# First feed-forward of a decoder block: modulation products, block sums of u and the depth of the weight split, moved in the order

## The chip, the cores and the metric

One core of a Trainium2 chip. The metric is device time in microseconds (us) of one execution of the program on that core. TensorE (PE, with its weight loads PEld) multiplies; VectorE (DVE), ScalarE (ACT) and GpSimd (POOL) compute beside it; SyncE (SP) issues nearly all loads, POOL the accumulating ones.

## The reference

One decoder block in float32, 512 tokens of width 1024. A vector c gives nine modulation vectors of 1024; three sublayers, each normed, shifted, scaled and gated by three of these, are added to the stream h, and a last norm ends it:

```python
cond = silu(c)
sh1, sc1, gt1, sh2, sc2, gt2, sh3, sc3, gt3 = split(cond @ w_ada + b_ada, 9)
u = rmsnorm(h, g1) * (1 + sc1) + sh1
h = h + 0.5 * gt1 * swiglu(u, w_ffn1_in, w_ffn1_out)     # (silu(a) * b) @ w_out, a, b = split(u @ w_in), D_FF = 2816
u = rmsnorm(h, g2) * (1 + sc2) + sh2
h = h + gt2 * token_mixing(u, ...)                       # pooling and dilated attention, gated
u = rmsnorm(h, g3) * (1 + sc3) + sh3
h = h + 0.5 * gt3 * swiglu(u, w_ffn2_in, w_ffn2_out)
return rmsnorm(h, g_final)
```

The change lies in the first swiglu.

## The kernel before, in words

**Layout.** Everything is transposed: features on the 128 partitions, the 512 tokens along the row. h lies in eight tiles H, u in eight pairs UH, UL. Each float32 operand is split into a high part, rounded to what a fast matmul takes (`hi`, on ACT), and the rest (`lo`, on DVE); a product is three matmuls: hi by hi, hi by lo, lo by hi.

**Weight chunks.** Weights come in chunks of 128 x 1024, loaded by SP (line 244) into a few buffers (raw0 to raw2, later also others that are idle: quarters of X, `kept1`, `G`) and split into a ring `whi`, `wlo` that holds seven chunks. `split_hi` makes, where a chunk is a difference of block weights, that difference on DVE (line 260), and the high part on ACT (line 321); `split_lo` the low part on DVE (line 335). For some chunks (`outer`) the low part is made otherwise: ACT writes the negative rounded copy into `wlo` (line 317), and POOL issues a load that adds the weights from memory to it (line 319). `look(n)` before each tile or product splits chunks until n stand ahead of the one in use; `take` hands the next one to TensorE. Chunks 0 to 7 are the startup's, 8 to 11 the plain pairs', 12 to 15 the first output part's, 16 to 22 the first block pair's seven products'.

**Stages of the first feed-forward.** The startup computes modulation rows 0 to 15 and norm, and the first eight tiles of u @ w_in (four pairs a, b, lines 1801 to 1805). Its end takes their results (`ffn_post`: the product silu(a) b into `kept` on DVE, line 671, the high part HI on ACT, line 680, the low part HK on DVE, line 681). Then two plain pairs, j = 4 and 5 (`ffn_pair`: two tiles each of 24 matmuls, lines 366 to 368). Then the first output part, eight tiles in four steps m = 0, 2, 4, 6, each tile added into H on DVE (line 1199). All further pairs go by a seven-product scheme on 2 x 2 blocks (Strassen's way; `duo`, two pairs at a time, from j = 6; `out_quad` for the output). It needs sums and differences of u's blocks (`u_steps`, lines 731 to 739: SH, SL from quarters of X; the last step overwrites parts of UH, UL) and of the weights' blocks (line 260). The sums of u wait in the list `todo` and are made one by one behind the H additions of the first output part; while `hold` is true, no weight difference is made ahead of time.

**Modulation rows.** Rows of w_ada (128 x 1024 each) are loaded by SP (line 381) and multiplied and summed on DVE (`ada_do`, line 389; `bg` does the next one and fetches more). Rows 16 to 23, the first feed-forward's gate, go beside the plain pairs from a pool of four buffers; `beside_out` closes that pool, opens the space of the u sums, and from then on rows go through the two buffers cs and AR, two per block pair, up to row 39.

**Order.** Each engine runs its instructions in the order in which this code issues them; nothing is reordered later. An instruction waits in its engine's queue until its inputs are there, and what is behind it waits too. Buffers are handed out in the order in which they come free, so a change in the order here exchanges raw buffers and quarters of X in the stages behind, too.

Of the kernel before, what the change touches and what calls it, by code (L numbers as in the profile page):

```python
# [125 lines left out]
PLAIN = {0: 6, 2: 2}  # L126
# [16 lines left out]
class Kernel:  # L143
# [279 lines left out]

    def beside(self, j, i):

        if self.nh == 4 and i in (2, 5):
            self.bg()

    def bg_fetch(self):
        while self.ada_ahead < min(self.ada_stop, self.ada_next + self.ada_depth) and self.ada_free != []:  # L430
# [342 lines left out]
    def duo(self, j, first):  # L773
# [32 lines left out]
        for i, (bank, u, start) in enumerate(((A, blk(lo4, T1), True), (B, S[0], True), (A, S[1], False),  # L806
                                              (C, blk(hi4, T1), False), (A, S[2], False), (B, S[3], False),
                                              (A, blk(hi4, T2), False))):
            if i == 6:
                v.tensor_tensor(c1, c1, u3, op=OP.add)  # L810
            self.look(3 + i // 3 if first else 5)
            self.product(bank, u, start)
            self.step()
            if i == 0:
                copy(C, A)
                if first:
                    first()
                    self.free.append(self.rawx[0])
            elif i == 1:
                copy(c1, r(B))  # L820
            elif i == 2:
                copy(c0, r(A))
            elif i == 3:
                silu(0, C)
            elif i == 4:
                copy(u3, r(A))
            elif i == 6:
                silu(1, A)
                v.tensor_tensor(c0, r(B), c0, op=OP.add)
            self.beside(j, i)  # L830
            if self.nh == 4 and j >= PARTS[-2][0] and self.todo:
                self.todo.pop(0)()
# [306 lines left out]
    def ffn(self, n, j, last=None):  # L1139
# [4 lines left out]
            self.banks, self.bi = list(self.B), 0  # L1144

        def beside():
            if n == 0:
                self.bg()
                if part == 0 or j == PLAIN[0] - 2:
                    self.bg()  # L1150

        for part, (k0, k1) in enumerate(PARTS[:-1]):
            while j < pairs_before(n, part):
# [3 lines left out]
                else:  # L1157
# [4 lines left out]
                    self.duo(j, last)  # L1162
                    last = None
                    j += 2
            if n == 0:
                last = self.beside_out(part) or last
            if part + 2 == len(PARTS):
                self.sums.close()
                if n:
# [13 lines left out]
            nk = k1 - k0  # L1183
            hk = [self.hh(k) for k in range(k0, k1)]
            for m in range(0, KT, 2):
                if m == 4:
                    self.bg_fetch()
                self.look(4 - m // 2)
                w = self.take()
                bs = [self.nb(), self.nb()]  # L1190

                for ka, kb in ((0, nk - 1), (nk - 1, nk)) if m == 0 else ():
                    for i in range(2):
                        for k in range(ka, kb):
                            self.mm3(bs[i], *w[nk * i + k], *hk[k], k == 0, k == nk - 1)
                for i, b in enumerate(bs):
                    for k in range(nk if m else 0):
                        self.mm3(b, *w[nk * i + k], *hk[k], k == 0, k == nk - 1)
                    v.scalar_tensor_tensor(self.H[m + i], b, gate[:, m + i:m + i + 1], self.H[m + i],
                                           op0=OP.mult, op1=OP.add)  # L1200
                    if self.todo:
                        self.todo.pop(0)()
                    if self.hold and not self.todo:
                        self.hold = False
                        self.look(2)
                self.step()
# [497 lines left out]
    def startup(self):  # L1704
# [99 lines left out]
            for (hi, lo), b in zip(w, banks):  # L1804
                M(b, lo, self.UH[k], start=False, stop=k == KT - 1)  # L1805
        self.ada_next = self.ada_ahead = 16
        self.ada_stop = 24
        self.bg_fetch()
        for j in range(FIRST):
            self.split(self.pos + j)  # L1810
            self.fetch()
            self.ffn_post(j, self.ffn_silu(j, banks[2 * j]), banks[2 * j + 1])


def constants():
# [55 lines left out]
```

## Time and profile before

| | us |
|---|---|
| median of three runs | 994.1 |
| lowest, highest | 989.12, 1396.78 |
| profiled execution | 993.37 |
| its span, first to last instruction | 991.6 |

| engine | busy us | share |
|---|---|---|
| PE | 977.8 | 99% |
| PEld | 921.3 | 93% |
| DVE | 830.4 | 84% |
| ACT | 591.5 | 60% |
| POOL | 95.6 | 10% |

The granted TensorE clock is 0.997 of full speed over the span. In lists in order of time the columns are the start in us from the span's beginning, the duration in us, the engine, the line, the operation and its tiles (written <- read); brackets give the idle time ahead and what ended it. Starts that lie closer than the durations mean pipelining. L770 is a block product, L366 to L368 a plain one.

### The profile page before, as it was taken

What the parts mean: (1) busy time and instruction counts of PE and PEld (TensorE: products, weight loads), DVE (VectorE), ACT (ScalarE), POOL (GpSimd) and SP (SyncE); (2) the same over time, 40 slices, a digit from 0 to 9 for tenths busy, and PEclk for the clock granted to TensorE, in tenths of its full rate; (3) what the DMA queues carried; (4) which work ended last, traced back from release to release, by engine and by line L of the source; (5) the groups of instructions that cost most, each with busy time, mean ns of one, the idle gap of its engine ahead of it and who ended that gap; (6) DMA issues with size and microseconds to landing.
All of it is one profiled execution on the core that took longest, in us unless ns stands there. A gap on an engine that the chain in (4) does not pass through costs nothing.

```text
span 991.6 us, 17667 instructions
## 1 busy us (share of the span) xinstructions
PE 977.8 (99%) x7106; PEld 921.3 (93%) x7106; DVE 830.4 (84%) x1246; ACT 591.5 (60%) x910; POOL 95.6 (10%) x107
## 2 busy tenths in 40 slices
PE   8999999999999999999999999999999999999997
PEld 7888999999999999889988888899999999999996
DVE  5979899999999877879666777479997988989876
ACT  5454687786868753333324333368876768577775
POOL 0000111111111100006200000000110010011001
PEclk9999999999999999999999999999999999999998
DMA  8959687877869822133265774346576566657622
GB/s 308 294 189 310 173 230 199 235 199 215 221 190 227 201 68 88 63 107 105 77 228 190 269 246 139 106 152 138 138 176 183 151 163 167 181 136 193 170 57 85
DMA packets 53636, 172.76 MB, mean 174 GB/s; under 512 B 6065, under 2 KB 11057, under 8 KB 53554
## 3 DMA queue, kind: packets, MB, share of 16 engines
q1 hardware_dynamic: 41778, 137.95, 40.6%
q0 software_dynamic: 11088, 33.04, 19.7%
q8 instruction: 55, 0.90, 0.4%
q10 hardware_dynamic: 688, 0.66, 0.2%
q14 instruction: 27, 0.22, 0.1%
HBM read 168.85 MB, written 2.77 MB: 173 GB/s over the span
## 4 chain that ended last, share of the span: by engine, by line
PE 94%; DVE 3%; ACT 1%; DMA 1%; issue 0%; DVEq 0%; ACTq 0%
PE bank L770 33%; PE bank L366 8%; PE bank L368 8%; PE bank L367 8%; PE bank L890 6%; PE bank L892 6%; PE bank L891 6%; PE bank L632 3%; PE bank L1801 1%; PE bank L1805 1%; PE bank L1803 1%; PE bank L1391 1%; PE bank L1572 1%; DMA wlo<-wf1i 1%; PE bank L1730 1%; PE bank L1573 1%
## 5 line engine op out<-in xcount | busy, mean ns | idle before, releaser
L335 DVE TENSOR_TENSOR wlo<-raw,whi 128x1024 fp32r<-128x1024 f32 (+5 forms) x117 | 121.6, 1053 | 38.4 <-ACT whi L321 38.1
L321 ACT ACTIVATE whi<-raw 128x1024 fp32r<-128x1024 f32 (+5 forms) x165 | 144.5, 895 | 10.3 <-DVE raw L260 6.3
L321 ACT ACTIVATE whi<-X 128x1024 fp32r<-128x1024 f32 (+3 forms) x101 | 97.0, 972 | 32.5 <-DVE X L260 32.1
L366 PE MATMUL bank<-UH,whi 128*128 128x512 f32 x240 | 97.4, 406 | 0.0
L335 DVE TENSOR_TENSOR wlo<-X,whi 128x1024 fp32r<-128x1024 f32 (+1 forms) x74 | 84.5, 1148 | 11.9 <-ACT whi L321 11.8
L368 PE MATMUL bank<-UH,wlo 128*128 128x512 f32 x240 | 93.6, 390 | 0.0
L367 PE MATMUL bank<-UL,whi 128*128 128x512 f32 x240 | 93.5, 390 | 0.0
L770 PE MATMUL bank<-UH,wlo 128*128 128x256 f32 x576 | 77.5, 277 | 1.7 <-DMA wlo<-wf1i 1.7
L770 PE MATMUL bank<-UH,whi 128*128 128x256 f32 x576 | 77.2, 276 | 0.0
L770 PE MATMUL bank<-UL,whi 128*128 128x256 f32 x576 | 77.2, 276 | 0.0
L770 PEld LDWEIGHTS bank<-UH,wlo 128*128 128x128 f32 x576 | 70.9, 188 | 1.9 <-DMA wlo<-wf1i 1.9
L770 PEld LDWEIGHTS bank<-UH,whi 128*128 128x128 f32 x576 | 70.9, 188 | 0.1
L770 PEld LDWEIGHTS bank<-UL,whi 128*128 128x128 f32 x576 | 70.8, 188 | 0.0
L890 PE MATMUL bank<-HI,whi 128*128 128x256 f32 x240 | 66.8, 278 | 0.0
L891 PE MATMUL bank<-HK,whi 128*128 128x256 f32 x240 | 66.4, 277 | 0.0
L892 PE MATMUL bank<-HI,wlo 128*128 128x256 f32 x240 | 66.4, 277 | 0.0
L890 PE MATMUL bank<-ut,whi 128*128 128x256 f32 x216 | 59.7, 277 | 0.0
L891 PE MATMUL bank<-G,whi 128*128 128x256 f32 x216 | 59.7, 277 | 0.0
L892 PE MATMUL bank<-ut,wlo 128*128 128x256 f32 x216 | 59.7, 277 | 0.0
L389 DVE SCALAR_TENSOR_TENSOR ada<-ada,cond 128x1024 f32<-128x1024 f32 (+1 forms) x49 | 57.5, 1197 | 1.8 <-DMA ada<-wada 1.6
L770 PE MATMUL bank<-SL,whi 128*128 128x256 f32 x432 | 58.5, 278 | 0.0
L770 PE MATMUL bank<-SH,whi 128*128 128x256 f32 x432 | 58.3, 277 | 0.0
(369 smaller groups left out, 2639.1 us busy)
## 6 DMA issues: line engine op xcount, KB each, us to landing
ada<-wada SPq DMA_DIRECT2D x47, 512.0 KB, 5.5
raw<-wmix SPq DMA_DIRECT2D x44, 512.0 KB, 4.2
raw<-wf1i SPq DMA_DIRECT2D x29, 512.0 KB, 7.2
raw<-wf2i SPq DMA_DIRECT2D x27, 512.0 KB, 5.7
wlo<-wf2i POOLq DMA_DIRECT2D x20, 512.0 KB, 5.6
raw<-wf1o SPq DMA_DIRECT2D x16, 512.0 KB, 5.5
AR<-wada SPq DMA_DIRECT2D x16, 512.0 KB, 4.5
X<-wf2i SPq DMA_DIRECT2D x14, 512.0 KB, 6.3
```

What stands on the lines that cost most here:

```text
L321: self.nc.scalar.activation(self.hi[:, y], r[:, x], AF.Copy)
L335: self.nc.vector.tensor_tensor(self.lo[:, y], r[:, x], self.hi[:, y], op=OP.subtract)
L366: M(ps, hi, uh, start=start, stop=False)
L367: M(ps, hi, ul, start=False, stop=False)
L368: M(ps, lo, uh, start=False, stop=stop)
L389: self.nc.vector.scalar_tensor_tensor(t[:, c], t[:, c], 1.0, self.cond[:, c], op0=OP.mult, op1=OP.mult, accum_out=o)
L632: M(banks[j][:, hs], w[j][k][x], (self.UH, self.UL)[y][k][:, hs], start=h == k == x == y == 0, stop=k == KT - 1 and x == 1, skip_group_che ...
L770: M(bank[:, p * HT:(p + 1) * HT], w[4 * p + k][x], u[k][y], start=start and x == y == p == k == 0, stop=x == 1 and k == 3, skip_group_chec ...
L890: M(o, hi, uh, start=start and m % 2 == 0 and k == 0, stop=False, skip_group_check=True)
L891: M(o, hi, ul, start=False, stop=False, skip_group_check=True)
L892: M(o, lo, uh, start=False, stop=k == 1, skip_group_check=True)
L1391: M(o, pt[:, blk * P:blk * P + P], v, start=i == 0, stop=i == len(srcs) - 1)
```

## The change

Three things move, all in the first feed-forward; nothing that is computed changes. Modulation rows 16 to 25 are now wanted before the pool closes (`ada_stop` 26): four of them, one each, on DVE between the kept product and its low part HK in the startup's end; four beside pair 4, two beside pair 5's first tile. Behind pair 5's second tile `beside_out` opens the sums' space, and the first three of u's sums are made there instead of behind H additions; the first block pair has no modulation rows, only a fetch of two. `look` in the block pairs of this feed-forward goes to four ahead in the first pair from its first product on (it was 3, 4, then 5), and in the output part to four ahead once `hold` has ended, which now comes after m = 2 instead of at m = 6.

```diff
--- before.py
+++ after.py
@@ -423,8 +423,11 @@
 
     def beside(self, j, i):
 
-        if self.nh == 4 and i in (2, 5):
-            self.bg()
+        if self.nh == 4:
+            if j > PLAIN[0] and i in (2, 5):
+                self.bg()
+            elif j == PLAIN[0] and i == 3:
+                self.bg_fetch()
 
     def bg_fetch(self):
         while self.ada_ahead < min(self.ada_stop, self.ada_next + self.ada_depth) and self.ada_free != []:
@@ -808,7 +811,7 @@
                                               (A, blk(hi4, T2), False))):
             if i == 6:
                 v.tensor_tensor(c1, c1, u3, op=OP.add)
-            self.look(3 + i // 3 if first else 5)
+            self.look((4 if self.nh == 4 else 3 + i // 3) if first else 5)
             self.product(bank, u, start)
             self.step()
             if i == 0:
@@ -1144,10 +1147,15 @@
             self.banks, self.bi = list(self.B), 0
 
         def beside():
+            nonlocal last
             if n == 0:
+                if self.ada_next == 26:
+                    last = self.beside_out(0)
+                    for _ in range(3):
+                        self.todo.pop(0)()
+                    return
                 self.bg()
-                if part == 0 or j == PLAIN[0] - 2:
-                    self.bg()
+                self.bg()
 
         for part, (k0, k1) in enumerate(PARTS[:-1]):
             while j < pairs_before(n, part):
@@ -1162,8 +1170,8 @@
                     self.duo(j, last)
                     last = None
                     j += 2
-            if n == 0:
-                last = self.beside_out(part) or last
+            if n == 0 and part:
+                self.beside_out(part)
             if part + 2 == len(PARTS):
                 self.sums.close()
                 if n:
@@ -1183,9 +1191,7 @@
             nk = k1 - k0
             hk = [self.hh(k) for k in range(k0, k1)]
             for m in range(0, KT, 2):
-                if m == 4:
-                    self.bg_fetch()
-                self.look(4 - m // 2)
+                self.look(4 - m // 2 if self.hold else 4)
                 w = self.take()
                 bs = [self.nb(), self.nb()]
 
@@ -1804,12 +1810,12 @@
             for (hi, lo), b in zip(w, banks):
                 M(b, lo, self.UH[k], start=False, stop=k == KT - 1)
         self.ada_next = self.ada_ahead = 16
-        self.ada_stop = 24
+        self.ada_stop = 26
         self.bg_fetch()
         for j in range(FIRST):
             self.split(self.pos + j)
             self.fetch()
-            self.ffn_post(j, self.ffn_silu(j, banks[2 * j]), banks[2 * j + 1])
+            self.ffn_post(j, self.ffn_silu(j, banks[2 * j]), banks[2 * j + 1], lambda low: (self.bg(), low()))
 
 
 def constants():
```

On DVE, at the startup's end (the first two results; `raw` chunks being split), before:

```order
L671 TENSOR_TENSOR kept_120<-sl,bank_98 128x512
L681 TENSOR_TENSOR HK<-kept_120,HI 128x512
L335 TENSOR_TENSOR wlo<-raw_66,whi 128x1024
L671 TENSOR_TENSOR kept_120<-u_549,bank_100 128x512
L681 TENSOR_TENSOR HK<-kept_120,HI 128x512
L335 TENSOR_TENSOR wlo<-raw_67,whi 128x1024
```

and now:

```order
L674 TENSOR_TENSOR kept_120<-sl,bank_98 128x512
L389 SCALAR_TENSOR_TENSOR ada,mod<-ada,cond 128x1024
L684 TENSOR_TENSOR HK<-kept_120,HI 128x512
L335 TENSOR_TENSOR wlo<-raw_66,whi 128x1024
L674 TENSOR_TENSOR kept_120<-u_552,bank_100 128x512
L389 SCALAR_TENSOR_TENSOR ada,mod<-ada,cond 128x1024
L684 TENSOR_TENSOR HK<-kept_120,HI 128x512
L335 TENSOR_TENSOR wlo<-raw_67,whi 128x1024
```

One modulation product stands between each kept product and its low part.

On DVE, from the second plain pair's kept product (kept_122 from bank_100) on (X are u's quarters, SL the low parts of their sums), before:

```order
L671 TENSOR_TENSOR kept_122<-u_671,bank_100 128x512
L1199 SCALAR_TENSOR_TENSOR H_72<-bank_101,mod,H_72 128x512
L731 TENSOR_TENSOR X<-X 128x1024
L1199 SCALAR_TENSOR_TENSOR H_73<-bank_102,mod,H_73 128x512
L731 TENSOR_TENSOR X<-X 128x1024
L1199 SCALAR_TENSOR_TENSOR H_74<-bank_103,mod,H_74 128x512
L739 TENSOR_TENSOR SL_715<-X,SH_713 128x1024
L1199 SCALAR_TENSOR_TENSOR H_75<-bank_104,mod,H_75 128x512
L731 TENSOR_TENSOR X<-X 128x1024
L1199 SCALAR_TENSOR_TENSOR H_76<-bank_97,mod,H_76 128x512
L739 TENSOR_TENSOR SL_720<-X,SH_719 128x1024
L1199 SCALAR_TENSOR_TENSOR H_77<-bank_98,mod,H_77 128x512
```

and now, from the last two modulation products of the plain pairs on:

```order
L389 SCALAR_TENSOR_TENSOR ada,mod<-ada,cond 128x1024 x2
L734 TENSOR_TENSOR X<-X 128x1024 x2
L742 TENSOR_TENSOR SL_720<-X,SH_718 128x1024
L674 TENSOR_TENSOR kept_122<-u_681,bank_100 128x512
L1205 SCALAR_TENSOR_TENSOR H_72<-bank_101,mod,H_72 128x512
L734 TENSOR_TENSOR X<-X 128x1024
L1205 SCALAR_TENSOR_TENSOR H_73<-bank_102,mod,H_73 128x512
L742 TENSOR_TENSOR SL_725<-X,SH_724 128x1024
L1205 SCALAR_TENSOR_TENSOR H_74<-bank_103,mod,H_74 128x512
L734 TENSOR_TENSOR X<-X 128x1024
L1205 SCALAR_TENSOR_TENSOR H_75<-bank_104,mod,H_75 128x512
L742 TENSOR_TENSOR SL_723<-X,SH_722 128x1024
```

Two sums and one low part have moved ahead of the kept product and of all H additions. The last low part now follows the fourth H addition, and the first weight difference comes right behind it; before, the list goes on with the last sum, the seventh H addition and the last low part ahead of that difference.

On ACT, from the negative copy of chunk 19 (kept_121) to that of chunk 21 (raw_66, two pieces), before:

```order
L317 ACTIVATE wlo<-kept_121 128x1024
L321 ACTIVATE whi<-kept_121 128x1024
L776 ACTIVATE bank_103<-bank_101 128x512
L736 ACTIVATE UH<-X 128x4x256
L321 ACTIVATE whi<-raw_68 128x1024
L776 ACTIVATE kept_120<-bank_102 128x2x256
L317 ACTIVATE wlo<-raw_66 128x256
L317 ACTIVATE wlo<-raw_66 128x768
```

and now:

```order
L317 ACTIVATE wlo<-kept_121 128x1024
L321 ACTIVATE whi<-kept_121 128x1024
L321 ACTIVATE whi<-raw_68 128x1024
L779 ACTIVATE bank_103<-bank_101 128x512
L739 ACTIVATE UH<-X 128x4x256
L317 ACTIVATE wlo<-raw_66 128x256
L317 ACTIVATE wlo<-raw_66 128x768
```

Chunk 20's high copy (raw_68) moved ahead of the bank copy, and the second bank copy (kept_120) behind chunk 21.

## Prediction

> **What bounds the kernel now.** I read the page first, then the waits of TensorE alone, then TensorE's own timeline at the one place that those waits name, then the chain of waits into that place, and last DVE, ACT and the DMA queues around it. The page says that TensorE is never far from busy:
>
> ```profile
> PE 977.8 (99%) x7106; PEld 921.3 (93%) x7106; DVE 830.4 (84%) x1246; ACT 591.5 (60%) x910; POOL 95.6 (10%) x107
> ```
>
> Of the span of 991.6 us only 13.8 us are without a matmul. TensorE's waits (us in total, times, longest) list nearly nothing after the start, and one alone in the part of the program that the change touches:
>
> ```profile
> PE bank L770 <- DMA wlo<-wf1i: 1.7, 1, 1.7
> ```
>
> TensorE's timeline (start, us, instruction) shows the second plain tile beginning at 69.02, and the products of the first block pair: the first starts at 107.09, the second at 109.92, so 2.83 us each, and the sixth stops after two of its low weights:
>
> ```profile
> 69.02 0.39 PE L366 MATMUL bank<-UH,whi 128*128 128x512 f32 x1
> ...
> 107.09 1.10 PE L770 MATMUL bank<-UH,whi 128*128 128x256 f32 x8
> ...
> 109.92 1.10 PE L770 MATMUL bank<-SH,whi 128*128 128x256 f32 x8
> ...
> 122.82 0.39 PE L770 MATMUL bank<-UH,wlo 128*128 128x256 f32 x2
> 124.95 0.96 PE L770 MATMUL bank<-UH,wlo 128*128 128x256 f32 x6 [1.75 <-DMA wlo<-wf1i]
> ```
>
> So TensorE would have gone on at 124.95 - 1.75 = 123.20. What it waited for is the second accumulating load of chunk 21 (r22, whose ring place wraps, hence two pieces). The chain of waits (start, us, what) follows that back to DVE:
>
> ```profile
> 106.50 1.24 DVE X L260
> ...
> 112.03 0.48 ACT bank L776
> 112.51 0.72 ACT UH L736
> 113.39 1.05 ACT whi L321
> 114.44 0.48 ACT kept L776
> 114.92 1.04 ACT wlo L317 x2
> ...
> 116.32 8.59 DMA wlo<-wf1i
> ```
>
> The reader is to see that the load's 8.59 us begin only when ACT has written the negative copy (L317), that ACT had four other things right before that copy, and that DVE makes its first weight difference (L260) only at 106.50, after all sums of u. Everything that this change can give back on TensorE is these 1.75 us; after 125 none of TensorE's waits lies in the first feed-forward.
>
> **The change part by part.** *Four modulation products beside the first pairs' results.* DVE there, in time order:
>
> ```profile
> 64.21 0.69 DVE L681 TENSOR_TENSOR HK<-kept,HI 128x512 fp32r<-128x512 f32 x1 [0.70 <-ACT HI L680]
> 65.16 1.23 DVE L335 TENSOR_TENSOR wlo<-raw,whi 128x1024 fp32r<-128x1024 f32 x1 [0.26 <-ACT whi L321]
> ...
> 82.43 0.68 DVE L671 TENSOR_TENSOR kept<-sl,bank 128x512 f32<-128x512 f32 x1
> ```
>
> ```profile
> 89.68 1.23 DVE L389 SCALAR_TENSOR_TENSOR ada<-ada,cond 128x1024 f32<-128x1024 f32 x1 [1.56 <-DMA ada<-wada]
> ...
> 92.49 1.21 DVE L731 TENSOR_TENSOR X<-X 128x1024 f32<-128x1024 f32 x1
> 93.63 0.74 DVE L1199 SCALAR_TENSOR_TENSOR H<-bank,mod,H 128x512 f32<-128x512 f32 x1
> 94.29 1.21 DVE L731 TENSOR_TENSOR X<-X 128x1024 f32<-128x1024 f32 x1
> ```
>
> From start to start a 1024-wide operation takes 1.14 us (92.49 to 93.63) and an H addition 0.66 (93.63 to 94.29); both figures serve below. A product of 1.14 us now stands in each idle 0.70 us ahead of HK and runs into the 0.26 ahead of the next split: at most 0.2 us of delay to chunk 9's split. That split ends at 65.16 + 1.23 = 66.39, and its chunk is the second plain tile's, which TensorE begins at 69.02. Cost zero; if that cover were gone it would be those 0.2 us, four times. The products' rows must have landed:
>
> ```profile
> 52.02 2.25 SPq L381 DMA_DIRECT2D ada<-wada  x3
> ...
> 73.73 4.56 SPq L381 DMA_DIRECT2D ada<-wada  x2
> ...
> 79.11 2.62 SPq L381 DMA_DIRECT2D ada<-wada  x2
> ...
> 86.89 0.39 SPq L381 DMA_DIRECT2D AR<-wada  x1
> ```
>
> ```profile
> DMA to landing us min/median/max: 4.5/5.9/7.0
> ```
>
> Rows 16 to 18 are issued by 54.3 and land by 61.3, ahead of their use at 63.4. Each later row now stands on SP ahead of a weight load: row 22 goes out at about 73.7, rows 23 and 24 when DVE has freed their buffers, row 25 at about 79.1. By 5.9 to 7.0 us rows 22 to 25 land at 79.6 to 86.1, where DVE wants them at 80.1 to 85.7. I take a wait of under 1 us on DVE, bounded by 0 and by the 8.45 us of the first rival.
>
> *The block sums of u from the last plain tile on.* DVE comes to the kept product of the first plain pair at 82.43, as before; the ending of the third eighth, 0.3 us, now stands ahead of it; it takes 0.6 and the split of chunk 14 behind it 1.14, to 84.5. Two products (rows 24, 25): 86.8. Two sums: 89.1. The low part of the first sum waits for ACT, which in the profile finishes chunk 16 late:
>
> ```profile
> 89.05 1.04 ACT L321 ACTIVATE whi<-raw 128x1024 fp32r<-128x1024 f32 x1
> ```
>
> With ACT free at 90.1 at the latest and 1.06 us for the copy, the low part begins at 91.15 and ends at 92.3; the kept product of the second pair follows (0.6): 92.9. Then four H additions with two sums and two low parts between them, 4 x 0.66 + 4 x 1.14 = 7.2: the sums end at 100.1, though not all of this wait need come, since chunk 16's load no longer stands behind two modulation rows on SP; without it 98.0. I take the middle, 99. So the first weight difference begins at 99 instead of 106.50, and the third (chunk 20's), which is behind two differences, two splits and two H additions, ends 4 x 1.14 + 2 x 0.66 + 1.14 = 7.0 us later, at 106.
>
> *Four chunks ahead.* On ACT, chunk 20's high copy now stands ahead of the copy of the first product's bank, and chunk 21's negative copy directly behind u's last copy; chunk 20's copy and the second product's bank copy (113.39 and 114.44 in the chain) no longer stand between. ACT has chunk 20 behind it at 106 + 1.05 = 107.1, which is 2.9 us before the first product ends (109.92, so its bank copy can run from about 110.0; I say 110.1). From there, by the chain: 0.48 for the bank, 0.88 for u's copy (112.51 to 113.39), and the negative copy starts at 111.5 instead of 114.92, 3.4 us earlier. POOL issues its transfer as far behind that as before, at 112.9 instead of 116.32.
>
> How long that load takes is the open size. SP now issues four loads within about 2 us of it: two weight chunks of the next output part, then modulation rows into cs and AR, the first of which went out before 87. Bounds from rows: 3.0 to 9.9 us for the accumulating loads of the rest of the stage, the first line below (min/median/max); the second and third are one such load of POOL's and the AR row that SP had issued before it:
>
> ```profile
> DMA to landing us min/median/max: 3.0/5.8/9.9
> ```
>
> ```profile
> AR<-wada SPq DMA_DIRECT2D x1, 512.0 KB, 15.0
> wlo<-wf1i POOLq DMA_DIRECT2D x1, 512.0 KB, 8.9
> ```
>
> ```profile
> 89.46 0.86 POOL L319 DMA_DIRECT2D wlo<-wf1i  x1 [4.10 <-ACT wlo L317]
> ```
>
> AR went out at 86.89 and landed at 101.9; POOL's load went out at 89.46 and landed at 98.4, so it overtook SP's backlog. I take 8.59 again, the row of this very transfer: 112.9 + 8.6 = 121.5, 1.7 us before 123.20. With 9.9 it is 122.8, still before. The stall goes whole: -1.75.
>
> [...] By strict order of issue it would be AR's 15.0 us, which is the second rival.
>
> *What is late next.* Chunk 22, the next on TensorE, needs the difference that DVE makes right behind u's last low part (about 113), so its split is over by 117 and TensorE wants it at 123.2. The first pair's two modulation products (2 x 1.14 us) are gone from DVE there, so the next pair's chunks come earlier too. The H additions of the fifth to eighth output tile now stand behind two differences and two splits, 4.6 us; their banks are next written in the second block pair, behind 126. The rows in cs and AR leave SP at about 114, land by 129 even with AR's 15.0, and are used behind the second pair's third product, ten products after 107.09, at about 135. Later stages only exchange buffers. None of this costs anything on TensorE.
>
> *Sum.* The profiled execution took 993.37 us, 1.77 more than its span. 993.37 - 1.75 = 991.6. The profiled time is 0.07% under the median of 994.1, whose nearest other run is 989.12.
>
> **The rivals.** *No change: the rows come late.* If row 25, out at 79.1, took AR's 15.0 us, it would land at 94.1 instead of being used at 85.65; DVE stands 8.45 us, and with it the splits and sums behind the row. The wait for ACT falls away, so the sums end at 98.0 + 8.45 = 106.5 and chunk 20's difference at 113.5. ACT is through with chunk 20 at 114.5 instead of being idle at 110.1, and chunk 21's negative copy starts 4.4 us late, at 115.9, where it was at 114.92: 993.4, with 1.0 on top, 994.4, at the worst. It begins to decide at a slip of 8.45 - 4.4 = 4.0 us and has eaten the gain 3.4 us further, at 7.4. For it: the 1.56 us wait at 89.68 shows that such rows were late once already, in the fullest stretch. Against: rows issued before 83 landed within 7.0.
>
> *Slower: the accumulating load drowns.* Its four neighbours now go out within about 2 us of it. Should it then take AR's 15.0 us, it would land at 112.9 + 15.0 = 127.9, a stall of 4.7 instead of 1.75: +2.95, so 996.3. It decides from a landing time of 124.95 - 112.9 = 12.05 us. For it: those neighbours. Against: no accumulating load of the profile took over 9.9.
>
> [...] In the stretch with the 1.75 us the granted clock (the 1.00) did not fall:
>
> ```profile
> 105.00:125.00 20.00, 18.25 (x149) 17.66 (x148) 18.59 (x20) 14.47 (x21) 2.66 (x3) 1.00 0.78 199
> ```
>
> [...]
>
> **How the numbers follow.** The forecast, stall gone and nothing in its place, gets 0.76: its only unknown size has 1.7 us of room. No change gets 0.13, the drowned load 0.05, and 0.06 is left for what I don't see, either way. The prediction is the forecast's 991.6. The runs themselves lie 5 us apart, far more than the change moves: the low end is the fastest run less the stall, 989.12 - 1.75 = 987.4, the high end the median with the first rival's worst, 994.1 + 1.0 = 995.1; the second rival stays outside. About 2% is what a measurement of this kernel can tell, and no case moves the time by as much as 0.5%: within 2% gets 0.97, slower 0.02 for a mishap, faster 0.01.
>
> **What would show it.** Right: TensorE's waits without the line for wlo from wf1i, first difference (L260) near 99, chunk 21's negative copy (L317, two pieces) near 111.5 and directly behind u's copy, TensorE busy from 105 to 125 without a gap. The first rival shows as a DVE wait for ada of several us between 80 and 95 with the differences back at 105 or later; the second as the wlo wait still there with the negative copy early. I am wrong if another wait of over 0.5 us appears on TensorE between 64 and 345, or if the span falls by clearly more than 2 us.

## The result

In 22 executions of each, the changed kernel takes 987.7 us in the median (985.38 to 991.59), the kernel before 991.34 us (988.48 to 994.95, and the one value of 1396.78 that the table before shows too). The ratio is 0.9974 with a 95% interval of 0.9963 to 0.9985: 2.6 us less, between 1.5 and 3.7. That is a change of 0.26%, far under the 2% that the prediction named, and the interval does not include 1. The measured time lies in the predicted range, near its low end of 987.4; the predicted 991.6 is 3.9 us too high. The profiled execution of the changed kernel took 991.59 us, its span 989.8.

The page's line of busy times, which answers to the one of before:

```profile
PE 977.3 (99%) x7106; PEld 921.1 (93%) x7106; DVE 829.4 (84%) x1246; ACT 590.8 (60%) x910; POOL 95.4 (10%) x107
```

TensorE's waits of the changed kernel (us in total, times, longest):

```profile
PE bank L1729 <- ACT cond L1727: 3.4, 1, 3.4
...
PE bank L773 <- ACT u L779: 0.5, 1, 0.5
```

The line for wlo from wf1i is gone. A short one on ACT's u is new; more on it below. DVE's and ACT's timelines around the first block product, and the landing times of the accumulating loads there (min/median/max):

```profile
99.55 1.23 DVE L260 TENSOR_TENSOR X<-raw,raw 128x1024 f32<-128x1024 f32 x1
...
105.68 1.22 DVE L260 TENSOR_TENSOR raw<-raw,raw 128x1024 f32<-128x1024 f32 x1
```

```profile
107.02 1.06 ACT L321 ACTIVATE whi<-raw 128x1024 fp32r<-128x1024 f32 x1 [1.93 <-DVE raw L260]
110.01 0.58 ACT L779 ACTIVATE bank<-bank 128x512 f32<-128x512 f32 x1 [1.93 <-PE bank L773]
110.50 1.05 ACT L739 ACTIVATE UH<-X 128x1024 fp32r<-128x1024 f32 x1
111.45 1.14 ACT L317 ACTIVATE wlo<-raw 128x256 fp32r<-128x256 f32 x2
```

```profile
DMA to landing us min/median/max: 5.2/5.3/8.2
```

The first weight difference stands at 99.55 (106.50 before), chunk 21's negative copy at 111.45 (114.92 before), right behind u's copy, and its load lands within 8.2 us. The row of the windows for the stretch from 105 to 125, and TensorE's timeline there (the first product, and the low weights of chunk 21, now eight matmuls without a break):

```profile
105.00:125.00 20.00, 20.00 (x168) 19.65 (x167) 15.68 (x18) 13.25 (x20) 2.95 (x4) 1.00 0.73 187
```

```profile
106.98 1.10 PE L773 MATMUL bank<-UH,whi 128*128 128x256 f32 x8
...
122.60 1.07 PE L773 MATMUL bank<-UH,wlo 128*128 128x256 f32 x8
```

TensorE is busy for all of the 20 us, 18.25 before. In what follows, the **stage** is the time from the first block product to the first matmul of the next norm's sums (L457 or L460), both read from TensorE's timeline. It is 236.67 us here and 238.16 in the first profile of before. It leaves out the startup and the later stages, so it tells kernels apart better than the span does.

### The profile page after: what moved, and what is told of

It reads as the page before. It is cut to its first block, busy times and chain, and to the rows that moved or that the text cites. A ratio compares the mean times of both kernels' runs of the same rounds, so it can differ in the third digit from the quotient of the medians.

```text
span 989.8 us, 17656 instructions
## 1 busy us (share of the span) xinstructions
PE 977.3 (99%) x7106; PEld 921.1 (93%) x7106; DVE 829.4 (84%) x1246; ACT 590.8 (60%) x910; POOL 95.4 (10%) x107
## 4 chain that ended last, share of the span: by engine, by line
PE 91%; DVE 5%; ACT 1%; DMA 1%; issue 1%; DVEq 0%; ACTq 0%
PE bank L773 32%; PE bank L366 8%; PE bank L367 8%; PE bank L368 8%; PE bank L893 5%; PE bank L895 5%; PE bank L894 5%; PE bank L635 3%; PE bank L1807 1%; PE bank L1811 1%; PE bank L1809 1%; PE bank L1397 1%; DMA X<-wf1i 1%; DVE wlo L335 1%; PE bank L1578 1%
## 5 line engine op out<-in xcount | busy, mean ns | idle before, releaser
L389 DVE SCALAR_TENSOR_TENSOR ada<-ada,cond 128x1024 f32<-128x1024 f32 (+1 forms) x51 | 60.0, 1198 | 0.6 <-DMA ada<-wada 0.5
L773 PE MATMUL bank<-SH,wlo 128*128 128x256 f32 x432 | 58.2, 277 | 0.0
```

Of the source, the lines that this page charges most:

```text
L389: self.nc.vector.scalar_tensor_tensor(t[:, c], t[:, c], 1.0, self.cond[:, c], op0=OP.mult, op1=OP.mult, accum_out=o)
L773: M(bank[:, p * HT:(p + 1) * HT], w[4 * p + k][x], u[k][y], start=start and x == y == p == k == 0, stop=x == 1 and k == 3, skip_group_chec ...
```

## Experiments

The three parts are called products (the modulation products in the startup's end), sums (u's block sums from the last plain tile on) and look (four chunks ahead).

### The kernel before once more

No edit.

> The kernel before, unchanged, for a second profile. Theory (the stall follows from the order of work on DVE and ACT ahead of chunk 21's accumulating load): TensorE's wait for wlo from wf1i is there again, 1.75 us give or take 0.5, with the negative copy near 114.9. Rival (the stall was a chance of one execution, a load that happened to land late): it is under 0.5 us or gone, and the change gained by chance.

TensorE's wait for wlo, and the windows before and during the half clock (us, busy times, granted clock third from last):

```profile
PE bank L770 <- DMA wlo<-wf1i: 2.0, 1, 2.0
```

```profile
122.59:126.01 3.42, 1.40 (x12) 1.21 (x11) 3.42 (x6) 2.02 (x4) 0.00 (x0) 1.00 0.95 327
126.01:129.42 3.41, 3.41 (x18) 3.41 (x17) 3.41 (x5) 1.63 (x2) 0.86 (x1) 0.50 0.32 55
```

The stall is there again, 2.02 us, and has a tail: from 126.01 to 129.42 the clock is halved, and 18 matmuls run there in place of more than 30. That costs another 1.7 us. The stage is 240.03. The execution that the prediction was made from had the same stall, 1.75 us, without the tail.

### The changed kernel once more

No edit.

> The changed kernel, unchanged, for a second profile. Theory: no wait for wlo from wf1i again; negative copy of chunk 21 near 111.5. The new 0.53 us wait of TensorE for ACT near 238 in the first profile was a chance of one execution (a load of X that took 10 us): gone or below 0.2 here, and the span about 0.5 us shorter for it. Rival (the exchanged buffers make that load late each time): the wait is there again, 0.4 to 0.7 us.

No wait on TensorE in the stage at all: neither for wlo nor for ACT's u. The stage is 235.86. So the 0.53 us of the first profile was of that execution alone. There it stood behind a late plain load of a weight chunk into X, which took 10.0 us where the second profile has 7.1. DVE's and TensorE's timelines show both ends of that chain:

```profile
215.64 1.23 DVE L260 TENSOR_TENSOR X<-X 128x1024 f32<-128x1024 f32 x1 [3.99 <-DMA X<-wf1i]
```

```profile
238.65 1.19 PE L773 MATMUL bank<-UH,whi 128*128 128x256 f32 x8 [0.53 <-ACT u L779]
```

### Only the look

```diff
-            self.look(3 + i // 3 if first else 5)
+            self.look((4 if self.nh == 4 else 3 + i // 3) if first else 5)
...
-                self.look(4 - m // 2)
+                self.look(4 - m // 2 if self.hold else 4)
```

on the kernel before.

> The kernel before with only the look-ahead of four (block pairs and output part) of the change. Theory: not enough. The sums of u end as late as before, so chunk 20's weight difference ends near 113.2 on DVE; its high copy on ACT now stands ahead of the bank copy, and the negative copy of chunk 21 comes at 115.5 instead of 114.9: TensorE's stall for wlo is 2.0 to 2.8 us, the span 0.3 to 1 us longer than before. Rival (the order on ACT alone is what helped): negative copy near 111.5 to 113, stall gone or under 0.5 us.

TensorE's waits and ACT's timeline (the first block product starts at 103.64, and ends with the second's start at 106.47):

```profile
PE bank L770 <- ACT bank L776: 2.0, 1, 2.0
PE bank L770 <- DMA wlo<-wf1i: 1.4, 1, 1.4
```

```profile
109.84 1.06 ACT L321 ACTIVATE whi<-raw 128x1024 fp32r<-128x1024 f32 x1 [1.26 <-DVE raw L260]
110.81 0.58 ACT L776 ACTIVATE bank<-bank 128x512 f32<-128x512 f32 x1
```

No gain: the waits come to 3.4 us, more than before, and the stage of 239.96 lies at the upper end of what before shows. The wait for wlo is shorter than expected, and the one for ACT's bank copy was not expected. The look puts chunk 20's high copy ahead of the first bank copy on ACT. With the differences still late, that copy waits for DVE until 109.84, and the bank copy, which could have run from 106.5, comes at 110.81. The third product writes this bank again and cannot start before 111.4. This deadline, 5.6 us behind the first product's start, is in no step of the prediction, nor in the expectation of this run.

### Products and sums, with the old look

```diff
-            self.look((4 if self.nh == 4 else 3 + i // 3) if first else 5)
+            self.look(3 + i // 3 if first else 5)
...
-                self.look(4 - m // 2 if self.hold else 4)
+                self.look(4 - m // 2)
```

on the changed kernel.

> The changed kernel with the look-ahead of before (3, 4, 5 in the first block pair; falling from 4 to 1 in the output part). Theory: not enough either. The sums end near 99, but with the small look-ahead no weight difference is made until the output part is over; the first difference comes at 107.5 to 108 behind the eighth H addition, and the negative copy at 115 or later: stall 2 to 3.5 us, no gain over before. Rival (the early sums are what helped): first difference near 99, negative copy by 113, stall under 0.5 us.

TensorE's waits:

```profile
PE bank L773 <- DMA wlo<-wf1i: 2.6, 1, 2.6
...
PE bank L773 <- ACT bank L779: 0.6, 1, 0.6
```

With 0.2 us for ACT's high copy TensorE's waits come to 3.5 us, the stage to 240.28. With the old look the first difference stands behind all eight H additions, at 104.02, 0.86 us after the first product's start (103.16); in the kernel before it stood 0.60 ahead. The early sums give back nothing without the look, which decides where the differences stand.

### Only the products

```diff
-            self.ffn_post(j, self.ffn_silu(j, banks[2 * j]), banks[2 * j + 1])
+            self.ffn_post(j, self.ffn_silu(j, banks[2 * j]), banks[2 * j + 1], lambda low: (self.bg(), low()))
```

on the kernel before.

> The kernel before with only the four modulation products beside the first pairs' results (rows 16 to 23 still end before the output part, sums and look-ahead as before). Theory: no gain. DVE reaches the second pair's kept product about 5 us earlier, but the sums still stand between the H additions, and those wait for TensorE's tiles; the first weight difference stays within 0.5 us of where it was against the first block product (0.6 us ahead of it), and the stall for wlo stays at 1.5 to 2.1 us. Rival (DVE's load was the limit, so freeing it is enough): difference 3 us or more earlier, stall under 0.5 us.

TensorE's wait for the load:

```profile
PE bank L770 <- DMA wlo<-wf1i: 1.4, 1, 1.4
```

TensorE's waits show the stall still there (and 0.2 us for a bank copy in the second block pair), DVE's timeline the first difference 0.60 us ahead of the first product, as in the kernel before. The negative copy comes 7.72 us behind that product's start, 7.73 before. The products alone move nothing. The wait of 1.4 us is just below the expected 1.5 to 2.1. The stage, 239.56, is 2.1 us more than 235.86 and these waits. Some 1.4 of that lie between 130 and 168 us, where groups of eight matmuls take 0.94 us each where 0.91 is usual; the mean granted clock of the execution is 0.997, as in the first execution of before, and the cause stays open.

### Sums and look, without the products

The kernel before with both edits of the look, and:

```diff
         def beside():
+            nonlocal last
             if n == 0:
                 self.bg()
-                if part == 0 or j == PLAIN[0] - 2:
-                    self.bg()
+                self.bg()
+                if self.ada_next == 24 and last is None:
+                    last = self.beside_out(0)
+                    for _ in range(3):
+                        self.todo.pop(0)()
...
-                last = self.beside_out(part) or last
+                if part:
+                    self.beside_out(part)
```

> The second and third part of the change without the first: the modulation products stay where they were in the kernel before (eight beside the plain pairs, the next two inside the first block pair), u's sums and the look are those of the changed kernel. Theory (the stall needs both the early sums and the look, and the products' place is worth little): DVE has two products more, 2 x 1.14 = 2.3 us, ahead of u's sums, so the first weight difference comes about 5 us ahead of the first block product instead of the 7.4 of the changed kernel; ACT had 1.93 us to spare ahead of the first bank copy, so that copy is at most 0.4 us late, chunk 21's negative copy comes 4.5 to 5.0 us behind the first block product's start, and TensorE waits neither for wlo nor for ACT's bank copy (0 to 0.3 us in all). Rival (all three parts are needed): rows 20 to 23 come late or the two products inside the first pair hold up the differences, and the two waits together are 1.0 us or more.

TensorE's wait, DVE's one wait between 84 and 112, and the windows around the stall:

```profile
PE bank L770 <- DMA wlo<-wf1i: 1.9, 1, 1.9
```

```profile
90.38 1.22 DVE L389 SCALAR_TENSOR_TENSOR ada<-ada,cond 128x1024 f32<-128x1024 f32 x1 [2.28 <-DMA ada<-wada]
```

```profile
122.49:125.90 3.41, 1.51 (x14) 1.31 (x12) 3.41 (x4) 2.55 (x3) 0.19 (x1) 1.00 0.64 227
125.90:129.32 3.42, 3.42 (x19) 3.42 (x18) 3.25 (x5) 0.41 (x1) 0.67 (x1) 0.50 0.60 95
```

My theory fell, and the rival held. The last of the eight rows was late by 2.28 us, the sums came behind it, and the first difference was 3.86 us ahead of the first product (103.34 against 107.20) where the changed kernel has 7.43. The negative copy came 6.04 us behind that product's start, not 4.47; an accumulating load took up to 10.3 us, and TensorE waited 1.90 us and went on at half clock. Stage 239.82. Without the 2.28 us the difference would have been 1.3 us behind the changed kernel's, less than the 1.93 us that ACT had to spare; that this would have been enough is worked out, not run. What the products' new place gives is that the last rows are fetched and used earlier, and all fourteen profiles bear that out: DVE's longest wait for a row between 55 and 100 us is 1.56 to 2.33 us in the six with the products in the old place, and at most 0.57 in the eight with the new one.

Put together (the wait is TensorE's in the first and second block pair of this stage):

| parts | wait, us | half clock behind it | stage, us |
|---|---|---|---|
| none (three executions) | 1.75; 2.0; 1.1 + 0.5 | no; yes; no | 238.16; 240.03; 238.16 |
| products | 1.4 + 0.2 | no | 239.56 |
| look | 2.0 + 1.4 | no | 239.96 |
| products, sums | 2.6 + 0.6 + 0.2 | no | 240.28 |
| sums, look | 1.9 | yes | 239.82 |
| all three (two executions) | 0 | no | 236.67; 235.86 |

No other combination that was run removes the stall. The sums alone, and the products with the look, were not run.

### Chunk 21's low part on DVE

```diff
         ffn(0, f1i, f1o, FIRST)
+        del self.outer[21]
```

on the kernel before: no accumulating load for chunk 21, and a split on DVE instead.

> The kernel before with one edit: the low part of chunk 21 is made on DVE like most others, not by negative copy and accumulating load. Theory (that load is the whole stall): TensorE's wait for wlo is gone, from the first block product to the first norm sum behind the stage 236.0 to 236.6 us instead of 238.2. Rival (DVE is too full there; the split takes the load's place as the late one): a wait of TensorE for DVE wlo of 1 us or more.

TensorE's wait, and ACT's timeline ahead of it:

```profile
PE bank L771 <- ACT bank L777: 2.2, 1, 2.2
```

```profile
129.68 1.06 ACT L322 ACTIVATE whi<-raw 128x1024 fp32r<-128x1024 f32 x1 [2.33 <-DVE raw L261]
...
132.17 1.14 ACT L322 ACTIVATE whi<-X 128x256 fp32r<-128x256 f32 x2
133.21 0.58 ACT L777 ACTIVATE bank<-bank 128x512 f32<-128x512 f32 x1
```

The wait for wlo is gone, and the stage is 238.34, as before: a wait of 2.19 us, which ends at 133.84, has taken its place. It is the same deadline one pair on, the third product's, with ACT held up by DVE's difference. Both expectations missed: the stall did not go without a successor, and the successor is a wait for ACT, not for DVE's wlo. The load was what TensorE waited for, but putting a split on DVE in its place is no gain while DVE stays behind. That the gain comes from an earlier DVE is tested by the slips below.

### More traffic ahead of the load

```diff
-            elif j == PLAIN[0] and i == 3:
+            elif j == PLAIN[0] and i == 0:
                 self.bg_fetch()
+                self.nc.sync.dma_start(self.tr, self.a["wada"][:P, :5 * P])
```

on the changed kernel: the rows into cs and AR, and a further load of 128 x 640 that nothing uses, are asked for behind the first block product's issue instead of the fourth's.

> The changed kernel with the two modulation rows for cs and AR fetched behind the first block product instead of the fourth, and one more load of 128 x 640 (not used) behind them: 1.35 MB that SP issues about 2 us ahead of chunk 21's accumulating load. It tests the second rival of the prediction. [...] Order of issue: the 1.35 MB, 3.4 us at 0.4 MB a us, come first, landing 11 us or more, stall 1.3 us or more.

```profile
101.22 0.43 SPq L381 DMA_DIRECT2D cs<-wada  x1
...
102.17 0.68 SPq L431 DMA_DIRECT2D tr<-wada  x1
```

```profile
103.96 0.86 POOL L319 DMA_DIRECT2D wlo<-wf1i  x1 [14.67 <-ACT wlo L317]
112.34 1.79 POOL L319 DMA_DIRECT2D wlo<-wf1i  x2 [7.52 <-ACT wlo L317]
```

```profile
DMA to landing us min/median/max: 5.4/5.5/8.1
```

SP's and POOL's timelines show the order of issue, the third view the landing times of the accumulating loads between 107 and 124: up to 8.1 us, 8.2 in the changed kernel. TensorE waits for nothing, and the stage is 235.86. But the run does not test what it was made for. The further traffic left SP from 101.22 on, some 10 us ahead of chunk 21's load (112.34) and not about 2, and both rows had landed by 108.6, before that load was issued (the third load's landing is not in the trace). What it shows is the accumulating load ahead of it, which did go out some 2 us behind this traffic, at 103.96: it took 8.6 us, against 5.5 for the one at 104.43 in the changed kernel, so 3 us longer. The 0.4 MB a us of the expectation is the rate that before has in its startup, 395 GB/s between 10 and 15 us.

The second rival is answered by the changed kernel itself. There SP issues its four loads from 112.84 to 114.56, and the large piece of chunk 21's load goes out among them, at 112.95; it took 8.2 us in both executions, far from the 12.05 from which that rival was to decide. The run with more traffic neither confirms this nor speaks against it.

### A slip on DVE: six, three and eight additions

```diff
                     last = self.beside_out(0)
+                    for _ in range(6):
+                        self.nc.vector.tensor_tensor(self.cs, self.U4[0][0], self.U4[0][1], op=OP.add)
```

on the changed kernel, with 6, 3 and 8. Each addition takes 1.14 us, and nothing uses what it writes.

> The changed kernel with six idle additions of 1024 on DVE (6.8 us, result not used) ahead of the sums of u. It tests the first rival, a DVE that is late. The prediction had the gain shrink from a slip of 4.0 us and gone at 7.4, so by it nearly the old time: stall about 1.3 us, for wlo alone. After the run with the look-ahead alone I expect more: the first bank's copy on ACT stands behind chunk 20, and the third product needs it; TensorE waits 1.5 to 2.5 us for ACT's bank copy, and for wlo another 0.3 to 1.4: 2.0 to 3.5 us together. If DVE's slip did not matter, both are 0.

TensorE's waits with six:

```profile
112.15 1.19 PE L773 MATMUL bank<-SH,whi 128*128 128x256 f32 x8 [2.13 <-ACT bank L779]
124.76 1.53 PE L773 MATMUL bank<-UH,wlo 128*128 128x256 f32 x6 [1.98 <-DMA wlo<-wf1i]
```

The stretches around the first wait and around the second:

```profile
107.86:111.27 3.41, 2.17 (x19) 1.97 (x17) 3.41 (x6) 1.48 (x2) 0.87 (x1) 1.00 0.78 161
111.27:114.68 3.41, 2.53 (x22) 2.53 (x23) 3.19 (x4) 3.41 (x7) 0.94 (x2) 1.00 0.68 138
121.51:124.92 3.41, 1.43 (x13) 1.23 (x12) 3.41 (x5) 2.84 (x3) 0.48 (x1) 1.00 0.98 344
124.92:128.34 3.42, 3.42 (x17) 3.42 (x18) 1.91 (x3) 0.11 (x1) 0.38 (x1) 0.50 0.72 141
```

Both deadlines are missed, 4.1 us together, more than the expected 2.0 to 3.5: the wait for wlo exceeds its 0.3 to 1.4, and chunk 21's load took 10.2 us here, not 8.2. Only the second wait has the half clock behind it, 0.50 from 124.92 to 128.34; around the first the clock stays at 1.00. Stage 242.48. With three:

> The changed kernel with three idle additions of 1.14 us each on DVE ahead of u's sums (3.4 us; nothing is left out of the result). With six of them the two waits came to 4.1 us. Theory (room before anything is felt: 0.6 us in DVE's own wait for SH, 1.93 us on ACT ahead of the first bank copy, 2.05 us from that copy's place to the third product, and some 1.4 us between the accumulating load's landing and its use): the differences come 2.8 us later than in the changed kernel, the negative copy 0.9 us later, and TensorE waits 0 to 0.5 us for the two together, all of it for wlo. Rival (the loss is proportional, about 0.6 us per us of slip): 2.0 us or more. By the prediction's own count a slip under 4.0 us costs nothing.

TensorE's wait with three:

```profile
PE bank L773 <- DMA wlo<-wf1i: 0.3, 1, 0.3
```

TensorE waits for wlo alone, 0.3 us; the negative copy is 0.91 us later against the first product than in the changed kernel (5.38 for 4.47), as the theory had it. Stage 236.41. With eight:

> The changed kernel with eight idle additions of 1.14 us each on DVE ahead of u's sums (nothing is left out of the result). With six of them TensorE waited 2.13 us for the first bank copy at 110.02 to 112.15 without any slow matmul behind it, and 1.98 us for wlo with 3.41 us at half clock behind it. [...] Stage from the first block product to the norm's sums: 236.1 + 4.4 + 1.7 + 0 to 0.7 = 242.2 to 242.9 us. Theory B (the half clock belongs to the wait for the load, not to idleness): the wait of 4.4 us is followed by full clock, stage 240.5 to 241.5 us.

TensorE's longest wait with eight, and the stretches in it and behind it:

```profile
PE bank L773 <- ACT bank L779: 3.6, 1, 3.6
```

```profile
111.05:114.46 3.41, 0.23 (x3) 0.04 (x1) 3.41 (x6) 1.48 (x3) 0.51 (x1) 1.00 0.76 120
114.46:117.87 3.41, 3.00 (x14) 3.00 (x15) 3.20 (x4) 3.41 (x7) 1.42 (x2) 0.50 0.70 144
```

The bank copy's wait is 3.59 us here, since another wait of 1.05 us, for chunk 17's high part, now stands ahead of it; that one I had not foreseen. Its end lies in a stretch at half clock, 0.50 from 114.46 to 117.87, which theory B of the expectation excludes. In the expected sum 4.4 is the 2.13 us with six additions and 2 x 1.14 more, against 3.59 and 1.05 here, and 1.7 is half of 3.41 us; that a half clock would come was an estimate from the runs with waits of 1.90 to 2.02 us. Stage 243.11, 0.2 above the foreseen 242.2 to 242.9.

The slip is how much nearer the first difference has come to the first product's start than in the changed kernel. The run without the products fits between (the last column is TensorE's wait, for the bank or its high part, and for wlo):

| run | slip of the first difference, us | negative copy later by | waits |
|---|---|---|---|
| three additions | 2.91 | 0.91 | 0 and 0.3 |
| without the products | 3.57 | 1.57 | 0 and 1.9 |
| six additions | 6.30 | 4.29 | 2.1 and 2.0 |
| eight additions | 9.10 | 7.09 | 4.6 and 0.4 |

Each time the copy is late by the slip less 2.0 us. That is the 1.93 us for which ACT waits for the bank (110.01, above): the whole room that the change has on ACT.

The load adds to it. Its large piece takes 8.2 us in the changed kernel and 9.4, 10.3, 10.2 and 9.9 in the four rows of the table, so a late copy was each time followed by a longer load as well; why is not shown.

### The kernel before a third time

No edit.

> The kernel before, unchanged, once more. It had a wait of 1.75 us for wlo without slow matmuls, and one of 2.02 us with 3.41 us at half clock. [...]

TensorE's waits:

```profile
PE bank L770 <- DMA wlo<-wf1i: 1.1, 1, 1.1
...
PE bank L770 <- ACT bank L776: 0.5, 1, 0.5
```

Here TensorE's wait for wlo was only 1.12 us, and one of 0.52 in the second block pair joined it. No half clock: the granted clock is 1.00 from 115 to 130. Stage 238.16.

The three executions also show what makes the stall longer or shorter. The negative copy comes 7.72, 7.72 and 7.73 us behind the first product's start, the same each time. The load behind it took 8.59 us in the first execution, and in the second (from its chain of waits) and the third (the longest of the landing times):

```profile
116.47 8.85 DMA wlo<-wf1i
```

```profile
DMA to landing us min/median/max: 5.2/5.8/8.0
```

The third load is 7.95 us by the trace. So the load took 0.26 us more and 0.64 less than in the first execution, and the wait was 0.27 more and 0.63 less: the order of work fixes where the load begins, and the time that the load takes then sets the size of the stall.

## Why the prediction was right, and where it was not

**The range: kept with some luck.** Its ends come from executions that lie 5 us apart, and 987.7 is only 0.3 us above the low one. What speaks for the mechanism is the stage and the waits, not the range.

**The bound and the stall: right.** The one wait it named is gone whole in both profiles of the changed kernel.

**Startup products at no cost: right.** Chunk 9's split starts at 65.06 us (65.16 before), and the products alone move nothing behind.

**The sums and differences: right.** 99.55 for "99", bounded by 98.0 and 100.1. Chunk 20's difference starts at 105.68 and ends at 106.9 for "106", 0.9 late.

**ACT and the load: right within 1.0 us.** Chunk 20 is done at 108.08 for 107.1, bank copy 110.01 for 110.1, negative copy 111.45 for 111.5, the load's large piece issued at 112.95 for 112.9, landing after 8.2 us for 8.59. Since chunk 20 was 1.0 us later than I had it, ACT's room was 1.93 us and not 2.9.

**What is late next: nearly right.** By the prediction's own words a new wait of over 0.5 us between 64 and 345 makes it wrong, and the first profile has one, of 0.53. The second has none. It was a late plain load and no consequence of the order, as far as two executions can tell. The other sign of being wrong, a span that falls by clearly more than 2 us, is a border case: the profiled spans fall by 1.8, the stage by 2.5, the timed runs by 2.6 with an interval that starts at 1.5.

**The sum: the term of 1.75 us was too small.** It was read from one execution. In three executions of before the stall was 1.75 us, 2.02 us with 1.7 more at half clock, and 1.12 + 0.52: 2.4 us in the mean, against 0.5 and nothing after. The stages say the same: 238.8 in the mean of three before, 236.3 in that of two after, 2.5 us less; the timed runs say 2.6 (1.5 to 3.7). The stage sums do not close exactly: 0.3 to 0.95 us, and 2.1 in the run with the products alone, stay beyond 235.86, the waits and the half clock. A part of this lies at the edges of a wait. It is counted from the end of the matmul ahead, 0.28 us after that one's start, where matmuls otherwise start 0.11 us apart, and the second matmul behind it starts 0.22 us after the first: 0.27 us in the first execution of before.

**The clock: the step that failed.** "In the stretch with the 1.75 us the granted clock (the 1.00) did not fall" was true of that execution and taken as if it were true of the stall: the 1.75 of the sum has no half clock in it. Waits of 2.02, 1.98 and 1.90 us (before a second time; six additions; sums and look) each had 3.41 us at 0.50 behind them, some 1.7 us more.

**The base: 2.0 us too high.** The predicted time stands on the profiled execution's 993.37, and the median of before is now 991.34. The rest of the miss of 3.9 is the gain: the medians differ by 3.64, the forecast had 1.75. Since the ratio gives 2.6, about 1 us of that difference may be the chance of two medians among times that lie over 6 us apart.

**The first rival: it did not come, and was priced too low.** DVE waited 0.48 us for a row in the first profile of the changed kernel and 0.57 in the second, under the 1 us that the prediction took. A slip of the differences was to cost nothing at first, to have eaten the gain at 7.4 us, and to end 1.0 us above before at the worst. Six additions, a slip of 6.30, make the stage 242.48, above all three executions of before. Three things were missing: the third product's wait for the first bank copy, which the look has put behind chunk 20, the half clock, and a load of 10.2 us where the prediction kept 8.59. The room was 2.0 us ahead of the negative copy, and some 0.6 us more in the load (with three additions the copy came 0.91 us late and TensorE waited 0.3).

**The second rival: it did not come.** Chunk 21's load took 8.2 us among its four neighbours. Accumulating loads above the prediction's bound of 9.9 do occur: 10.2 and 10.3 for this one (six additions; without the products), and 11.05 for the one that goes out at 88.90 in the changed kernel. None reaches the 12.05 from which the rival was to decide, but the margin is smaller than the prediction had it.

## What to carry to other kernels

Where TensorE is never idle for long, price a stall by more than its length: read the clock in the stretches behind it in several executions, since the same stall cost 1.75 us in one execution here, and 2.02 with some 1.7 more at half clock in another. When work is put ahead of something in an engine's queue, list every reader of what now comes later, such as the product that writes the same bank next, and count the room to each. Check in the profile that an experiment's disturbance stands where it was meant to stand: a load that was asked for earlier may have landed before what it was to disturb. A change of several parts may have no part that helps alone; compare by the stage in which the change lies when the span scatters more than the gain.

## What the runs showed of the hardware

**Behind some waits the clock halves.** In four executions 3.41 us at a granted clock of 0.50 followed TensorE's wait, or began ahead of its end: from 126.01 in the second execution of before, from 124.92 with six additions, from 125.90 with sums and look, and from 114.46 with eight additions. In the first and the last of these the stretch behind, from 129.42 and from 117.87, is at 1.00 again. 14 to 19 matmuls ran in each of the four, where 31 to 33 run in as long a stretch without a wait at 1.00. Waits, and what followed:

| execution | TensorE's wait, us | half clock behind it |
|---|---|---|
| before, first | 1.75 | no |
| before, second | 2.02 | yes |
| before, third | 1.12 | no |
| look only | 1.99 and 1.40 | no |
| products and sums | 2.60 | no |
| chunk 21 on DVE | 2.19 | no |
| six additions | 2.13 and 1.98 | no; yes |
| sums and look | 1.90 | yes |
| eight additions | 3.59 | yes |

The length of the wait does not decide: behind 2.60 us the clock stayed at 1.00, behind 1.90 it fell to 0.50. What decides was not shown. The stretches around the 2.60 us:

```profile
119.19:122.61 3.42, 1.52 (x14) 1.32 (x12) 3.42 (x5) 2.02 (x3) 0.00 (x0) 1.00 1.05 311
122.61:126.02 3.41, 2.71 (x23) 2.71 (x24) 3.41 (x4) 2.41 (x3) 0.86 (x1) 1.00 0.56 207
126.02:129.43 3.41, 3.41 (x32) 3.41 (x31) 2.22 (x4) 3.22 (x6) 1.02 (x2) 1.00 0.89 149
```

So the same stall cost 1.75 us in one execution of before, and 2.02 with some 1.7 more in another.

**The startup takes 4 us more or less by chance.** The first weight matmul started between 15.88 and 17.04 us in eight of the fourteen profiled executions, and between 19.58 and 20.02 in the other six, of both kernels. TensorE's timeline of a long startup (before), the last matmuls of the norm and the first weights:

```profile
17.53 2.67 PE L1730 MATMUL bank<-H,ones 128*128 128x128 f32 x12
19.95 2.08 PE L1801 MATMUL bank<-UH,whi 128*128 128x512 f32 x8
```

And of a short one (the changed kernel's second):

```profile
15.23 1.50 PE L1736 MATMUL bank<-H,ones 128*128 128x128 f32 x12
16.99 2.09 PE L1807 MATMUL bank<-UH,whi 128*128 128x512 f32 x8 [0.26 <-ACT UH L489]
```

The same twelve matmuls take 2.67 or 1.50 us. Why they differ was not shown. The difference is larger than what this change gives, and most of the scatter of the times of one kernel may be this; that was not measured apart.
